# Layer 1's attention with scores turned round: keys on the partitions, exponentials in place, no transposes of probabilities

## The chip, the cores and the metric

The kernel runs on one core of a Trainium2 chip. The metric is the device time of one execution in microseconds (us), the median of several runs. A core has five engines, each of which works through its own instructions in order and waits for the others by semaphores: PE (matrix products, whose weight loads the profile lists apart as PEld), DVE (vector work), ACT (functions such as the exponential), POOL (a second vector engine) and SP (issues most DMA transfers here). Products land in PSUM, eight banks of 512 float32 columns on 128 partitions; everything else lies in SBUF.

## What is computed

Two layers over 1024 latent tokens (a grid of 16 x 64) and 256 context tokens, 1024 features wide, in float32. Layer 0 mixes by a gated MLP and a neighbourhood attention, layer 1 by a grouped-query attention, and each layer ends in a gated MLP with a short convolution. The change lies in layer 1's attention alone:

```python
def gqa_attend(q, k, v):
    bn, lq, hq, dh = q.shape
    hkv = k.shape[2]
    qg = q.reshape(bn, lq, hkv, hq // hkv, dh)
    s = jnp.einsum('bqhgd,bkhd->bhgqk', qg, k).astype(jnp.float32) * (dh ** -0.5)
    p = jax.nn.softmax(s, axis=-1).astype(v.dtype)
    return jnp.einsum('bhgqk,bkhd->bqhgd', p, v).reshape(bn, lq, hq * dh)
```

There are 16 query heads, 4 key/value heads and 64 features a head. The queries are the 1024 latent tokens, the keys the 1024 latent and the 256 context tokens, 1280 in all. Queries and keys have been normalised and rotated before.

## The kernel before

**Operands.** `odd_in` projects the tokens and writes queries, keys and values to DRAM. A query or key is kept as a sum of two numbers of the shorter type that PE takes at its fast rate (`F32R`), hi and lo. `qP` holds, for each head, the 64 hi features on partitions 0 to 63 and the 64 lo features on partitions 64 to 127. `kP` holds a first set in which both halves of the partitions are the key's hi part (`k1`), and a second in which both are its lo part (`k2`). So the product of q with `k1` plus the product of q with `k2` is the whole product of sums. `load_keys` brings `k1`, `k2` and the values `Vs` of one key/value head to SBUF: two heads near the end of `odd_in`, two at the beginning of the attention. `load_q` brings four query heads for 256 tokens.

**Tiles.** `odd_attn` goes through 128 tiles. A tile is one head and 128 queries, with the queries on the partitions: four stretches `p` of 256 queries, 16 heads in each, two tiles `q` for each head. Step n of the loop writes, in this order and with the matrix, vector and scalar engines bound to it (`in_order`):

- `scores` of tile n: for 512, 512 and 256 keys one product with `k1` and one with `k2` (line 1605); a copy of each piece to SBUF on DVE that also yields its maximum (line 1607); then the maximum of the three (line 1611), one exponential over all 1280 columns on ACT that also yields their sum (line 1612), and on POOL the reciprocal of that sum as a power (line 1613) and a diagonal matrix of the reciprocals (line 1619).
- `turns` of tile n - 3: ten transposes of 128 x 128 on PE (line 1634) and three copies out of PSUM, two on ACT and one on DVE (line 1636), which set the keys on the partitions.
- a quarter of the `values` of an earlier pair of heads: products of the turned probabilities with `Vs` (line 1651), in plain float32, which the trace lists as two records a product. Before the last quarter, `sums` multiplies a matrix of ones with the diagonals (line 1663), which sets each query's reciprocal on the 64 partitions of its head, and after it DVE multiplies the values by them (line 1654) and SP stores the result to `yT1`.

PSUM is split into four banks for scores, three for transposes and sums, and one for values.

**Beside it.** `down_sums` (called `ts`) prepares sums of layer 1's last weights: 11 times it loads two pieces into one tile, subtracts four times on POOL (line 611) and stores the tile. A step of it is taken at every second tile; the tile has one buffer. Near the end, at tile 118 and the seven after it, `out_load` brings the finished half of `yT1` back and splits it on POOL (lines 407 and 408) for the output projection that follows (lines 317 to 319).

Of the kernel before, what the change touches and what calls it, by code (L numbers as in the profile page):

```python
# [9 lines left out]
F32 = mybir.dt.float32  # L10
# [7 lines left out]
P = 128  # L18
# [37 lines left out]
class Net:  # L56
# [1515 lines left out]
    def load_keys(self, pool, kv):  # L1572
        res = []
        for tag, off in (("k1", 0), ("k2", 4)):
            x = self.t(pool, [P, S], f"{tag}_{kv}", 1, F32R)
            self.nc.sync.dma_start(x.bitcast(F32), self.kP[:, off + kv])
            res.append(x)
        x = self.t(pool, [P, NT, 64], f"Vs_{kv}", 1)
        self.nc.sync.dma_start(x, self.vP[:, kv])
        self.KV[kv] = (*res, x)  # L1580
# [6 lines left out]

    def odd_attn(self, es):
        nc, tc = self.nc, self.tc
        with tc.tile_pool(name="ga", reuse_waits="tile", bufs=2) as gp, self.banks(turn=4, one=3, out=1):  # L1590

            def scores(tl):

                pt = tl["pt"] = self.t(gp, [P, S], "pt", 6)
                mm = self.t(self.sp, [P, 3], "mm", 6)
                ng = self.t(self.sp, [P, 1], "ng", 6)
                sm = self.t(self.sp, [P, 1], "sm1", 6)
                ri = self.t(self.sp, [P, 1], "ri", 6)
                kv, q = tl["kv"], tl["q"]
                qs = tl["Q"][:, tl["h"] % 4, q * P:(q + 1) * P]  # L1600

                def keys(i, ps, c0, w):
                    ps = ps[:, :w]
                    for ki, kk in enumerate(self.KV[kv][:2]):
                        nc.tensor.matmul(ps, qs, kk[:, c0:c0 + w], start=(ki == 0), stop=(ki == 1))  # L1605

                    nc.vector.tensor_scalar(pt[:, c0:c0 + w], ps, 1.0, NEG, op0=ALU.mult, op1=ALU.max, accum_out=mm[:, i:i + 1])  # L1607

                def last():
                    keys(2, self.t(self.bt, [P, 512], "b1"), T, C)  # L1610
                    nc.vector.tensor_reduce(ng, mm, axis=AX.X, op=ALU.max, negate=True)  # L1611
                    nc.scalar.activation(pt, pt, AF.Exp, bias=ng, accum_out=sm)  # L1612
                    nc.gpsimd.tensor_tensor(ri, sm, self.mone, op=ALU.pow)  # L1613

                    x = tl["h"] % 2
                    if x == 0 and q == 0:
                        self.dg = self.t(gp, [P, 2, 256], "dg", 4)
                    tl["dg"] = self.dg
                    nc.gpsimd.tensor_scalar(self.dg[:, x, q * P:(q + 1) * P], self.ident, ri, None, op0=ALU.mult)

                return [lambda i=i: keys(i, self.t(self.bt, [P, 512], "b1"), 512 * i, 512) for i in range(2)] + [last]

            def turns(tl):

                x, q, pt = tl["h"] % 2, tl["q"], tl["pt"]
                if x == 0 and q == 0:
                    self.pT = self.t(gp, [P, 2, NT, 256], "pT", 2)
                pT = tl["pT"] = self.pT

                def batch(b0):  # L1630
                    m = min(4, NT - b0)
                    tb = self.bank()
                    for i in range(m):
                        nc.tensor.transpose(tb[:, i * P:(i + 1) * P], pt[:, (b0 + i) * P:(b0 + i + 1) * P], self.ident)  # L1634
                    e = nc.vector.tensor_copy if b0 == 4 else nc.scalar.copy
                    e(pT[:, x, b0:b0 + m, q * P:(q + 1) * P], tb[:, :m * P].rearrange("p (a b) -> p a b", a=m))  # L1636

                return [lambda b0=b0: batch(b0) for b0 in (0, 4, 8)]

            def values(tl):  # L1640

                p, h, kv, pT = tl["p"], tl["h"], tl["kv"], tl["pT"]
                box = {}

                def part(i0, i1):
                    if i0 == 0:
                        box["po"] = self.t(self.by, [P, 512], "by")
                    po = box["po"][:, :256]
                    for i in range(i0, i1):
                        for x in range(2):  # L1650
                            nc.tensor.matmul(po[x * 64:x * 64 + 64], self.KV[kv][2][:, i, :], pT[:, x, i, :], start=(i == 0), stop=(i == NT - 1))  # L1651
                    if i1 == NT:
                        ya = self.t(gp, [P, 256], "ya", 4)
                        nc.vector.tensor_tensor(ya, po, box["rb"], op=ALU.mult)
                        nc.sync.dma_start(self.yT1[h // 2][:, p * 256:(p + 1) * 256], ya)

                def sums():

                    tb = self.bank()[:, :256]
                    for q in range(2):  # L1660
                        for x in range(2):
                            c = slice(q * P, (q + 1) * P)
                            nc.tensor.matmul(tb[x * 64:x * 64 + 64, c], self.ones, tl["dg"][:, x, c], start=True, stop=True)
                    box["rb"] = self.t(gp, [P, 256], "rb", 2)
                    nc.scalar.copy(box["rb"], tb)

                cuts = (0, 3, 5, 8, NT)
                return [(sums if b == NT else None, lambda a=a, b=b: part(a, b)) for a, b in zip(cuts, cuts[1:])]

            tiles = [dict(p=p, h=h, kv=h // 4, q=q, j=p * 16 + h) for p in range(4) for h in range(16) for q in range(2)]  # L1670
            pend, n0, Qn = [], None, self.Q
# [3 lines left out]
            for n in range(len(tiles) + 5):  # L1675
                sc, tu = [], []
                if n < len(tiles):
                    tl = tiles[n]
                    if n % 8 == 0:
                        Q = Qn  # L1680
                    if n % 8 == 3 and n + 5 < len(tiles):
                        nx = tiles[n + 5]
                        Qn = self.load_q(gp, nx["p"], nx["h"])
                    if n % 2:
                        self.steps(ts, 1)
                    if n in (1, 6):
                        self.load_keys(gp, 2 + n // 6)
                    if tl["p"] == 3 and tl["h"] == 11 and tl["q"] == 0:

                        self.es_g.close()  # L1690
                        xp = es.enter_context(tc.tile_pool(name="xq", reuse_waits="tile", bufs=1, side="right"))
                        xm = self.xm_tiles(xp)
                        n0 = n
                    if n0 is not None and n - n0 < 8:
                        self.out_load(xm, n - n0, self.yT1, 0, HF, self.t(gp, [P, 512], "raw", 1), "pp")
                    tl["Q"] = Q
                    sc = scores(tl)
# [119 lines left out]
```

## Time and profile before

| | us |
|---|---|
| three runs | 3074.65, 3075.59, 3079.21 |
| median | 3075.59 |
| the profiled execution | 3070.96 |
| its span, first to last instruction | 3069.2 |
| layer 1's attention, first score product to last value product | 1769.9 to 2279 |

A profile shows one execution. A row of a group names the line, the engine, the operation, what is written from what, the shape, the number of instructions, their busy time in us and the mean of one in ns; behind the bar at the right stands how long the engine had been idle before them, and what ended it. A row of the timeline begins with the start and the length in us; rows of the same kind that follow each other are merged, and "x8" gives their number. A row of windows gives the length of the stretch, then the busy time and number of instructions for PE, PEld, DVE, ACT and POOL, PE's granted clock as a share of the full one, the share of DMA time, and GB/s. PE's listed lengths include the way through the array, so that neighbours overlap; the distance of two starts tells what a product costs in a row.

### The profile page before, as it was taken

The numbers are of one execution on the slowest core, as the hardware profiler recorded it, in microseconds if no ns is written. First come the engines' busy times: TensorE is split into PE (matmuls) and PEld (weight loads), VectorE is DVE, ScalarE is ACT, GpSimd is POOL, SyncE is SP. The second block draws the span as 40 slices with busy tenths as digits, with TensorE's granted clock in tenths as the row PEclk, the third lists the DMA queues.
The fourth block names the chain that finished last, engine by engine and source line by source line (L and its number), as shares of the span: only waits on it lengthen the run. The fifth ranks groups of instructions, "written<-read, shape, count | busy, mean of one in ns | idle before, by whom it ended". The sixth has DMA issues, their size and how long they took to land. (4 is left out here: it accounts for less than half of the span.)

```text
span 3069.2 us, 45832 instructions
## 1 busy us (share of the span) xinstructions
PE 2926.8 (95%) x16819; PEld 2354.1 (77%) x16819; DVE 2127.8 (69%) x3397; ACT 1406.5 (46%) x2407; POOL 1439.8 (47%) x1532
## 2 busy tenths in 40 slices
PE   7999988998999999999989999999999899999997
PEld 6768956676888888878779977777777678888785
DVE  4441245468766666798997776666656988788998
ACT  4211156374433333344466566666636344444443
POOL 3541046446333333266665766433344744442767
PEclk9999999999999999999999999999999899999998
DMA  9685453363323322553154554200033122224542
GB/s 347 220 285 178 126 178 96 125 220 113 107 95 115 122 90 106 190 170 129 54 196 121 171 213 172 76 31 23 28 122 138 55 89 83 83 82 158 189 145 82
DMA packets 221120, 408.56 MB, mean 133 GB/s; under 512 B 27216, under 2 KB 119376, under 8 KB 212960
## 3 DMA queue, kind: packets, MB, share of 16 engines
q1 hardware_dynamic: 198192, 390.10, 37.1%
q10 hardware_dynamic: 22704, 15.55, 1.7%
q8 instruction: 132, 2.16, 0.3%
q14 instruction: 92, 0.75, 0.1%
HBM read 300.65 MB, written 104.92 MB: 132 GB/s over the span
## 5 line engine op out<-in xcount | busy, mean ns | idle before, releaser
L1607 DVE TENSOR_SCALAR_CACHE_REDUCE pt<-b 128x512 f32<-128x512 f32 (+1 forms) x384 | 229.7, 599 | 136.3 <-PE b L1605 134.9
L459 POOL TENSOR_TENSOR sw<-wraw,wraw 128x512 f32<-128x512 f32 x44 | 60.1, 1366 | 469.0 <-DVE wlo L122 469.0
L122 DVE TENSOR_TENSOR wlo<-wraw,whi 128x1024 fp32r<-128x1024 f32 (+1 forms) x160 | 213.4, 1338 | 84.7 <-ACT whi L116 83.9
L116 ACT CAST whi<-sw 128x1024 fp32r<-128x1024 f32 x88 | 92.2, 1048 | 338.1 <-PE by L497 241.3
L1605 PE MATMUL b<-k,Q 128*128 128x512 f32 (+1 forms) x768 | 244.8, 403 | 0.8 <-DVE pt L1607 0.8
L116 ACT CAST whi<-wraw 128x1024 fp32r<-128x1024 f32 (+1 forms) x160 | 157.3, 988 | 188.9 <-PE b L308 107.1
L1612 ACT ACTIVATE pt<-pt,ng 128x1280 f32<-128x1280 f32 x128 | 174.8, 1365 | 109.8 <-DVE ng L1611 107.6
L498 PE MATMUL by<-xb,wlo 128*128 128x512 f32 x528 | 209.9, 398 | 6.6 <-DVE wlo L122 6.6
L496 PE MATMUL by<-xb,whi 128*128 128x512 f32 x528 | 212.1, 402 | 3.3 <-DVE z L475 1.8
L475 DVE TENSOR_TENSOR z<-by,z 128x512 f32<-128x512 f32 x176 | 120.8, 687 | 133.9 <-POOL z L475 84.0
L497 PE MATMUL by<-xb,whi 128*128 128x512 f32 x528 | 210.3, 398 | 2.5 <-DVE xb L122 2.5
L122 DVE TENSOR_TENSOR xb<-xb,xb 128x512 fp32r<-128x512 f32 (+2 forms) x184 | 167.6, 927 | 23.4 <-ACT xb L116 20.6
L1634 PEld LDWEIGHTS b<-ident,pt 128*128 128x128 f32 x1280 | 154.7, 140 | 36.4 <-DVE pT L1636 1.4
L1634 PE MATMUL b<-ident,pt 128*128 128x128 f32 x1280 | 181.2, 272 | 0.5 <-ACT pT L1636 0.4
L116 ACT CAST xb<-xb 128x512 fp32r<-128x512 f32 (+2 forms) x184 | 103.2, 567 | 168.4 <-PE by L870 61.6
L122 DVE TENSOR_TENSOR wlo<-sw,whi 128x1024 fp32r<-128x1024 f32 x88 | 128.0, 1455 | 65.6 <-ACT whi L116 64.8
L611 POOL TENSOR_TENSOR ts<-ts 128x512 f32<-128x512 f32 x88 | 116.8, 1337 | 110.5 <-DMA ts<-in_w_down_dram 95.7
L1651 PE MATMUL by<-pT,Vs 128*64 128x256 f32 x1280 | 165.9, 389 | 0.0
L1613 POOL TENSOR_TENSOR ri<-sm,mone 128x1 f32<-128x1 f32 x128 | 72.6, 568 | 181.9 <-ACT pt L1612 134.6
L732 POOL TENSOR_TENSOR y<-y,wraw 128x512 f32<-128x512 f32 x72 | 115.1, 1620 | 85.4 <-DVE wraw L732 54.1
L1636 ACT COPY pT<-b 128x512 f32<-128x512 f32 (+1 forms) x256 | 120.7, 474 | 65.6 <-PE b L1634 64.0
L496 PE MATMUL by<-xm,whi 128*128 128x512 f32 x352 | 142.6, 405 | 6.8 <-ACT z L525 3.2
(302 smaller groups left out, 9146.7 us busy)
## 6 DMA issues: line engine op xcount, KB each, us to landing
wraw<-in_w_up_t_dram SPq DMA_DIRECT2D x89, 512.0 KB
awr<-in_w_ada_dram SPq DMA_DIRECT2D x44, 1024.0 KB
ts<-in_w_down_dram SPq DMA_DIRECT2D x44, 512.0 KB
tD<-ts SPq DMA_DIRECT2D x22, 1024.0 KB
xm<-tD SPq DMA_DIRECT2D x88, 256.0 KB
hid<-o SPq DMA_DIRECT2D x43, 512.0 KB
xm<-in_w_down_dram SPq DMA_DIRECT2D x66, 256.0 KB
xb<-hid SPq DMA_DIRECT2D x66, 256.0 KB
```

What stands on the lines that cost most here:

```text
L116: nc.scalar.copy(hi, src)
L122: nc.vector.tensor_tensor(lo, src, hi.bitcast(F32), op=ALU.subtract)
L475: add = lambda o, x, y, e=V: e.tensor_tensor(o, x, y, op=ALU.add)
L496: nc.tensor.matmul(o, W[0][:, k, :], hi[k], start=(k == 0), stop=False)
L497: nc.tensor.matmul(o, W[0][:, k, :], lo[k], start=False, stop=False)
L498: nc.tensor.matmul(o, W[1][:, k, :], hi[k], start=False, stop=(k == 3))
L1605: nc.tensor.matmul(ps, qs, kk[:, c0:c0 + w], start=(ki == 0), stop=(ki == 1))
L1607: nc.vector.tensor_scalar(pt[:, c0:c0 + w], ps, 1.0, NEG, op0=ALU.mult, op1=ALU.max, accum_out=mm[:, i:i + 1])
L1612: nc.scalar.activation(pt, pt, AF.Exp, bias=ng, accum_out=sm)
L1634: nc.tensor.transpose(tb[:, i * P:(i + 1) * P], pt[:, (b0 + i) * P:(b0 + i + 1) * P], self.ident)
L1636: e(pT[:, x, b0:b0 + m, q * P:(q + 1) * P], tb[:, :m * P].rearrange("p (a b) -> p a b", a=m))
L1651: nc.tensor.matmul(po[x * 64:x * 64 + 64], self.KV[kv][2][:, i, :], pT[:, x, i, :], start=(i == 0), stop=(i == NT - 1))
```

## The change

The unit of work becomes a block of four query heads (one key/value head `g`) and 128 queries: 32 blocks instead of 128 tiles. The score products are turned round: a chunk of 128 keys is the fixed operand, the four heads' queries (4 x 128 columns) stream through, and the result has the keys on the partitions, as the value products want it.

A maximum over the keys can no longer be taken from such a product. So `maxima` computes, for each head, the product of q with `k1` only, queries on the partitions, into three PSUM banks, and one reduction on DVE over 1280 columns gives the negated maximum. `rounded` copies the four to the shorter type on ACT; `shift` turns and spreads them over the partitions by four products with an identity, and ACT copies the upper half into `q2`, a second query operand whose lower half is q's hi part, loaded by a DMA of its own. `k2` now has its lo part on partitions 0 to 63, a row of ones on partition 64 and zeros below (two memsets on POOL). So the second score product adds lo times hi and takes off the maximum; lo times lo is left out. The exponential reads PSUM, has no bias and gives no sum.

The sum over the keys is formed from the ten chunks of exponentials: POOL adds chunks 0 to 4 (`first`, four additions), DVE adds 5 and 6 to 7 and 8 (`second`), then folds that, adds chunk 9 and POOL's part (`third`); two products with ones (`sums`) spread it over the 64 partitions of each head. DVE takes the reciprocal and multiplies (`result`). The transposes, their copies, the diagonals and POOL's powers are gone. PSUM is split into one buffer of three banks for the maxima, three banks for scores and shifts, two for values and sums.

Within a step the parts are written for four blocks: the block itself (`b`), the next two (`b1`, `b2`) and the one before (`last`). `ts` takes two steps a block; the load back for the output projection goes to blocks 29 to 31.

```diff
     def load_keys(self, pool, kv):
-        for tag, off in (("k1", 0), ("k2", 4)):
-            x = self.t(pool, [P, S], f"{tag}_{kv}", 1, F32R)
-            self.nc.sync.dma_start(x.bitcast(F32), self.kP[:, off + kv])
+        hi, lo = (self.t(pool, [P, S], f"{tag}_{kv}", 1, F32R) for tag in ("k1", "k2"))
+        self.nc.sync.dma_start(hi.bitcast(F32), self.kP[:, kv])
+        self.nc.sync.dma_start(lo[0:64].bitcast(F32), self.kP[0:64, 4 + kv])
+        self.nc.gpsimd.memset(lo[64:P].bitcast(F32), 0.0)
+        self.nc.gpsimd.memset(lo[64:65].bitcast(F32), 1.0)
...
+            def maxima(b, h):
+                ps = self.t(self.b2, [P, 1536], "b2")
+                for c, w in ((0, 512), (512, 512), (T, C)):
+                    nc.tensor.matmul(ps[:, c:c + w], b["q1"][:, h], self.KV[b["g"]][0][:, c:c + w], start=True, stop=True)
+                nc.vector.tensor_reduce(b["ng"][:, h:h + 1], ps[:, :S], axis=AX.X, op=ALU.max, negate=True)
...
+            def shift(b):
+                ps = self.t(self.bt, [P, 512], "b1")
+                for h in range(4):
+                    nc.tensor.matmul(ps[:, h * P:(h + 1) * P], b["mr"][:, h:h + 1].to_broadcast([P, P]), self.identr, start=True, stop=True)
+                nc.scalar.copy(b["q2"][64:P], ps[64:P].rearrange("p (h q) -> p h q", h=4))
+
+            def scores(b, k):
...
+                for i in range(2):
+                    nc.tensor.matmul(ps.rearrange("p (h q) -> p h q", h=4), self.KV[b["g"]][i][:, c], b[f"q{i + 1}"], start=(i == 0), stop=(i == 1))
+                nc.scalar.activation(b["pT"][:, k], ps, AF.Exp)
...
+            def sums(b):
+                for i in range(2):
+                    nc.tensor.matmul(out(b["po"][:, 256:], i), self.ones, two(b["acc"][:, 0], i), start=True, stop=True)
+
+            def first(b):
+                pT = b["pT"]
+                x = b["part"] = self.t(gp, [P, 512], "part", 2)
+                nc.gpsimd.tensor_tensor(x, pT[:, 0], pT[:, 1], op=ALU.add)
+                for k in (2, 3, 4):
+                    nc.gpsimd.tensor_tensor(x, x, pT[:, k], op=ALU.add)
+
+            def second(b):
+                b["acc"] = self.t(gp, [P, 2, 512], "acc", 2)
+                nc.vector.tensor_tensor(b["acc"], b["pT"][:, 5:7], b["pT"][:, 7:9], op=ALU.add)
+
+            def third(b):
+                x = b["acc"]
+                for y in (x[:, 1], b["pT"][:, 9], b["part"]):
+                    nc.vector.tensor_tensor(x[:, 0], x[:, 0], y, op=ALU.add)
+
+            def result(b):
+                rb = self.t(gp, [P, 256], "rb", 2)
+                nc.vector.reciprocal(rb, b["po"][:, 256:])
+                ya = self.t(gp, [P, 256], "ya", 4)
+                nc.vector.tensor_tensor(ya, b["po"][:, :256], rb, op=ALU.mult)
...
+            for h in range(4):
+                maxima(blocks[0], h)
+            rounded(blocks[0])
+            for h in range(2):
+                maxima(blocks[1], h)
+            shift(blocks[0])
+            for n in range(len(blocks) + 1):
...
+                if b2:
+                    begin(b2)
+                self.steps(ts, 2)
...
+                if b:
+                    scores(b, 0)
+                if last:
+                    second(last)
+                    values(last, 5, NT)
+                if b1:
+                    maxima(b1, 2)
+                if last:
+                    third(last)
+                if b:
+                    for k in (1, 2, 3, 4):
+                        scores(b, k)
+                    first(b)
+                if b1:
+                    maxima(b1, 3)
+                    rounded(b1)
+                if b:
+                    scores(b, 5)
+                if last:
+                    sums(last)
+                if b:
+                    values(b, 0, 5)
+                if b1:
+                    shift(b1)
+                if b2:
+                    maxima(b2, 0)
+                if last:
+                    result(last)
+                if b:
+                    for k in (6, 7, 8, 9):
+                        scores(b, k)
+                if b2:
+                    maxima(b2, 1)
```

More of the change, by code (lines that the diff above doesn't have):

```diff
@@ L1572, in load_keys @@
     def load_keys(self, pool, kv):
-        res = []
-        for tag, off in (("k1", 0), ("k2", 4)):
-            x = self.t(pool, [P, S], f"{tag}_{kv}", 1, F32R)
-            self.nc.sync.dma_start(x.bitcast(F32), self.kP[:, off + kv])
-            res.append(x)
+        hi, lo = (self.t(pool, [P, S], f"{tag}_{kv}", 1, F32R) for tag in ("k1", "k2"))
[3 more added lines that the diff above has]
+        self.nc.gpsimd.memset(lo[64:65].bitcast(F32), 1.0)
         x = self.t(pool, [P, NT, 64], f"Vs_{kv}", 1)
         self.nc.sync.dma_start(x, self.vP[:, kv])
-        self.KV[kv] = (*res, x)
+        self.KV[kv] = (hi, lo, x)
     def load_q(self, pool, p, h, bufs=2):
@@ L1589, in odd_attn @@
         nc, tc = self.nc, self.tc
[L1590 to L1671, printed above, removed]
@@ L1674, in odd_attn @@
             pinned.enter_context(self.in_order(nc.tensor, nc.vector, nc.scalar))
[L1675 to L1697, printed above, removed]
-                if 0 <= n - 3 < len(tiles):
-                    tu = turns(tiles[n - 3])
-                before, after = pend.pop(0) if pend else (None, None)
-                if before:
-                    before()
-                for f in [x for y in zip(sc[:2], tu[:2]) for x in y] + tu[2:] + sc[2:] if sc and tu else sc + tu:
-                    f()
-                if after:
-                    after()
-                if 0 <= n - 3 < len(tiles) and tiles[n - 3]["h"] % 2 and tiles[n - 3]["q"] == 1:
-                    pend += values(tiles[n - 3])
@@ L1709, in odd_attn @@
-            for before, after in pend:
-                if before:
-                    before()
-                after()
+            xp = None
+            begin(blocks[0])
+            begin(blocks[1])
+            self.load_keys(gp, 2)
+            for h in range(4):
[5 more added lines that the diff above has]
+            for n in range(len(blocks) + 1):
+                b, b1, b2, last = was(n), was(n + 1), was(n + 2), was(n - 1)
+                if n == 0:
+                    self.load_keys(gp, 3)
+                if b2:
+                    begin(b2)
+                self.steps(ts, 2)
+                if n == 29:
+                    self.es_g.close()
+                    xp = es.enter_context(tc.tile_pool(name="xq", reuse_waits="tile", bufs=1, side="right"))
+                    xm = self.xm_tiles(xp)
+                if n >= 29:
+                    for k in range(3 * (n - 29), min(KD, 3 * (n - 28))):
+                        self.out_load(xm, k, self.yT1, 0, HF, self.t(gp, [P, 512], "raw", 2), "pp")
+                if b:
[31 more added lines that the diff above has]
+                    maxima(b2, 1)
```

31 lines of the change are left out of this document (added).

## The prediction

> **What bounds the kernel now.** I read the busy times on the page first, then the engine windows over layer 1's attention (1770 to 2280 us), then PE's timeline inside it.
>
> ```profile
> PE 2926.8 (95%) x16819; PEld 2354.1 (77%) x16819; DVE 2127.8 (69%) x3397; ACT 1406.5 (46%) x2407; POOL 1439.8 (47%) x1532
> 1769.80:2280.00 510.20, 504.66 (x3661) 373.43 (x3660) 338.14 (x1066) 315.43 (x555) 222.84 (x321) 0.99 0.24 85
> 1950.00:2050.00 100.00, 100.00 (x744) 73.91 (x742) 68.58 (x218) 63.48 (x112) 31.03 (x53) 1.00 0.08 25
> ```
>
> The reader is to see that PE (first figure behind the length) is idle for 5.5 us of this stage and not at all in its middle, with DVE and ACT near two thirds and DMA at 0.08. So PE's own work is the bound, and every microsecond taken from PE counts until another engine makes PE wait. PE's timeline:
>
> ```profile
> 2000.65 0.61 PE L1663 MATMUL b<-dg,ones 128*64 128x128 f32 x8
> 2001.18 0.73 PE L1605 MATMUL b<-k,Q 128*128 128x512 f32 x2
> 2001.75 0.60 PE L1634 MATMUL b<-ident,pt 128*128 128x128 f32 x4
> 2002.11 0.71 PE L1605 MATMUL b<-k,Q 128*128 128x512 f32 x2
> 2002.65 0.82 PE L1634 MATMUL b<-ident,pt 128*128 128x128 f32 x6
> 2003.23 0.48 PE L1605 MATMUL b<-k,Q 128*128 128x256 f32 x2
> 2003.63 1.08 PE L1651 MATMUL by<-pT,Vs 128*64 128x256 f32 x8
> 2004.65 0.74 PE L1605 MATMUL b<-k,Q 128*128 128x512 f32 x2
> ...
> 2007.11 1.52 PE L1651 MATMUL by<-pT,Vs 128*64 128x256 f32 x12
> 2008.55 0.73 PE L1605 MATMUL b<-k,Q 128*128 128x512 f32 x2
> ```
>
> Starts count here, since listed lengths overlap. A tile (one head, 128 queries) takes 3.47 us with 8 value records and 3.90 with 12; with one group of sums (0.53) four tiles take about 15.2, and 32 such blocks 486 us. The transposes are 0.36 + 0.58 = 0.94 of each tile. Value records: 1.02 for 8, 1.44 for 12, so 0.107 each and 0.17 for a group.
>
> **The change, part by part.** PE first. The price of a long run of the score kind of product (512 and 256 columns) stands in other stages:
>
> ```profile
> 2254.54 0.39 PE L317 MATMUL by<-whi,xm 128*128 128x512 f32 x1
> ...
> 2257.34 0.39 PE L317 MATMUL by<-whi,xm 128*128 128x512 f32 x1
> ...
> 1768.73 0.28 PE L319 MATMUL by<-whi,xb 128*128 128x256 f32 x1
> ...
> 1769.44 0.28 PE L319 MATMUL by<-whi,xb 128*128 128x256 f32 x1
> 1769.56 0.46 PE L1513 MATMUL b<-identr,xb 128*128 128x128 f32 x4
> ```
>
> Twelve products lie between the first two (0.234 each), six between the others (0.118). A new block (four heads, 128 queries) has 20 score products, 4.68; maxima 8 x 0.234 + 4 x 0.118 = 2.34; 40 value records in two groups, 4.62; sums, 4 records, 0.43; shift about 0.4; two switches back, 0.2. Together 12.7 against 15.2: the transposes' 3.76 go, the maxima's 2.34 come, and longer runs save the rest. The shift's four products are bounded by four transposes of that width (0.46, the last row) and eight sums records (0.53), and below by 0.2; 0.4 is near both. Scores read q with a stride; their pairs now take up to 0.57, so 0.234 to 0.285 a product, and I take the long run. The high end adds some 0.5 a block to the path below.
>
> The other engines:
>
> ```profile
> L1636 DVE COPY pT<-b 128x512 f32<-128x512 f32 x128 | 87.8, 686 | 12.0 <-PE b L1634 12.0
> L1636 ACT COPY pT<-b 128x512 f32<-128x512 f32 x128 | 73.7, 575 | 13.5 <-PE b L1634 12.0
> L1654 DVE TENSOR_TENSOR ya<-by,rb 128x256 f32<-128x256 f32 x32 | 13.6, 425 | 18.2 <-PE by L1651 14.5
> L1312 DVE TENSOR_REDUCE ng<-b 128x1 f32<-128x256 f32 x16 | 6.0, 420 | 2.0 <-PE b L1302 2.0
> L1323 ACT ACTIVATE pt<-sc,ng 128x640 f32<-128x640 f32 x64 | 52.5, 824 | 7.6 <-DVE ng L1309 7.6
> L1279 POOL MEMSET bias<- 128x256 f32 x12 | 3.2, 310 | 114.4 <-DMA qD<-t 102.2 <-DMA VD<-h 6.6 <-issue 5.6
> 2002.85 0.69 DVE L1607 TENSOR_SCALAR_CACHE_REDUCE pt<-b 128x512 f32<-128x512 f32 x1 [0.20 <-PE b L1605]
> 2503.39 1.22 DVE L575 TENSOR_TENSOR o<-o,o 128x1024 f32<-128x1024 f32 x1
> 2833.14 0.69 DVE L122 TENSOR_TENSOR wlo<-xm,wlo 128x512 fp32r<-128x512 f32 x1
> 2833.74 0.69 DVE L122 TENSOR_TENSOR whi<-xm,whi 128x512 fp32r<-128x512 f32 x1
> ```
>
> ACT: ten exponentials of 512 at 0.58 (the copy; at most 0.82, the 640 row), the shift's copy and a tiny one: 6.6 to 9 us a block, hidden under PE's 12.7. `rounded` waits for the fourth maximum, and exponentials 5 to 9 queue behind it; the values before the shift cover that. DVE: a maximum over 1280 columns is 420 + 4 x 266 = 1.48 (266 is 686 less 420); 1.73 by the 0.69-us row's 1.35 ns an element. `second` is 1.22, `third` three adds of 0.68 that follow from each other, 2.1. An add that waits for nothing starts 0.08 before the last one's end (0.60 apart, 0.69 long). [...] DVE sums to 10.1, under PE. POOL loses its power and diagonal work and gains four adds a block. Its eight memsets are 1.55 each by the 256-wide row; `k2` is needed only after the lead-in, which hides the first two pairs; uncovered, 3 to 6 us once. SP issues 32 small q2 loads and twice the stores, and a block's loads stand behind the stores of the block before, which wait for `result`; DMA at 0.08 hides them, since q is wanted some 10 us after issue. If it were late, the third and fourth maxima of a block would wait for it.
>
> **The path within a block.** PE runs in a written order, so the added wait of `sums` for `third` holds back all behind it: five value chunks, the shift, two maxima, scores 6 to 9. Round the loop: sums 0.6 with the group, values 2.14, shift 0.5, maximum 0.59, scores 1.87, maximum 0.59, score 0.47, values 2.41, maximum 0.59, hand-over 0.20 (the row above), reduction 1.40, `third` 2.10, hand-over 0.1: **13.55 us**. PE idles 0.85 of it in front of `sums`.
>
> Then what POOL does meanwhile. POOL's four adds (`first`) read chunks 0 to 4 as ACT makes them. Let t be the end of the third maximum's products on PE. Score 1 is streamed at t + 0.47, its exponential done at t + 1.25, POOL starts at t + 1.35; `third` is ready at t + 0.20 + 1.40 = t + 1.6. Both read two operands each. How such adds share the time shows late in the kernel:
>
> ```profile
> 2904.69 1.74 POOL L681 TENSOR_TENSOR xb<-xb,a 128x512 f32<-128x512 f32 x1
> 2905.20 1.78 DVE L122 TENSOR_TENSOR wlo<-xm,wlo 128x512 fp32r<-128x512 f32 x1
> 2906.38 1.74 POOL L681 TENSOR_TENSOR xb<-a,a 128x512 f32<-128x512 f32 x1
> 2906.90 1.77 DVE L122 TENSOR_TENSOR xb<-a,xb 128x512 fp32r<-128x512 f32 x1
> 2908.08 1.74 POOL L681 TENSOR_TENSOR a<-a,xb 128x512 f32<-128x512 f32 x1
> ```
>
> The same DVE add takes 1.78 here and 0.69 above: one add of POOL and one of DVE go by turns, 1.70 a pair. [...] By whole lengths a pair would be 1.29 + 0.60 = 1.89, and the total some 8 us more than by the row.
>
> So `third` waits until POOL's first add is through (1.29 long in the next fence, t + 2.6), and two more pairs follow: its last add starts at t + 6.0 and ends at t + 6.7 instead of t + 3.7. That is 3.0 us, PE's stall grows to about 3.9, and the block takes **16.55**. Whether POOL waits for its chunk alone or for all chunks written ahead of it is read from the weight sums, whose two subtractions read two halves of one tile:
>
> ```profile
> 1829.75 1.29 POOL L611 TENSOR_TENSOR ts<-ts 128x512 f32<-128x512 f32 x1 [4.20 <-DMA ts<-in_w_down_dram]
> 1831.82 1.28 POOL L611 TENSOR_TENSOR ts<-ts 128x512 f32<-128x512 f32 x1 [0.79 <-DMA ts<-in_w_down_dram]
> ```
>
> The second waits again, for its own half: a reader waits for its piece. In every other one of the first 22 blocks these subtractions stand ahead of `first` and wait for a load issued in that block (4.20 above), so `first` comes after `third`; there I take half of one encounter, 14.1.
>
> **Lead-in.** Six maxima share one PSUM buffer: 0.59 + 0.20 + 1.48 + 0.1 = 2.37 each. PE is nearly idle then, and this is its clock (last figure but two of a window) in such a gap:
>
> ```profile
> 1773.72 0.51 PE L1513 MATMUL b<-identr,xb 128*128 128x128 f32 x4 [2.01 <-DVE xb L122]
> 1776.43 0.72 PE L1513 MATMUL b<-identr,xb 128*128 128x128 f32 x4 [2.20 <-DVE xb L122]
> ...
> 1774.00:1776.00 2.00, 0.23 (x3) 0.09 (x2) 1.34 (x4) 0.99 (x2) 0.85 (x1) 0.81 0.99 257
> 1776.00:1778.00 2.00, 0.78 (x5) 0.62 (x5) 1.10 (x4) 0.59 (x1) 0.00 (x0) 0.50 0.80 271
> ```
>
> With some products at half clock I take 16 us up to the first score (14 to 18).
>
> **Sum.** After: 16, then 10.5 for the first block (nothing to finish), 10 x 14.1, 21 x 16.55, and -3 for maxima that the last blocks lack, net of the last block's finish, which the output projection covers as it does now: 512. Before: 486 + 5.5 idle = 491.5. The difference is **+20.5 us**. The profiled execution took 3070.96 us for a span of 3069.2, so it becomes 3091.5; it lies 4.6 under the median of the three runs, 3075.59, on which I put the forecast: **3096**. Its own range is 3082 (shift and lead-in at their low ends, no encounter in the ten blocks) to 3121 (score pairs, reductions and lead-in at their high ends).
>
> **Rivals.**
> 1. *No turns, so faster.* If POOL's first add starts only past t + 3.0, when `third` has issued its last add, nothing collides: every block takes 13.55, the stage 16 + 10.5 + 31 x 13.55 - 3 = 443.5, so 48 less: 3028. [...] For it: ACT's exponentials could be slower than the copy, or POOL could wait for chunk 4 (t + 3.1). Against: the half-tile rows. It decides where the mean block passes (491.5 - 16 - 10.5 + 3) / 31 = 15.1.
> [...]
> 3. *The stall lowers the clock.* A stall of 3.9 is as long as the gap before 0.50 in the rows above (two waits with four products between). If sums and values then ran at half clock, 2.7 us come on top in 21 blocks: 3153.
> 4. *About even*: one collision instead of three, near 15.1 a block.
>
> That the transposes stay is no case; the diff leaves no call of them.
>
> **Chances.** Forecast 0.30, dear reciprocal 0.20, clock 0.04: slower 0.54. No turns 0.36: faster. Even 0.10. About 0.2% (6 us) is what a measurement can tell from no change. The range 3030 to 3130 reaches into both sides and leaves out the cheap end of rival 1 and rival 3.
>
> **What would show it.** PE: blocks of 12.7 us of work, a stall of 3 to 4 in front of the sums released by DVE's last add in late blocks (right), or under 1 (rival 1). DVE: adds of `third` at 1.7 while POOL's run, or 0.68. [...] PEclk under 1.0 in mid-stage means rival 3. I am wrong from the ground up if products of the new shapes are not 0.234, or if the stage downstream moves.

## The result and the profile after

| | us, median of the runs | range |
|---|---|---|
| before | 3075.17 | 3074.65 to 3079.21 |
| after | 3177.12 | 3174.36 to 3179.81 |

The ratio is 1.0329, with an interval from 1.0311 to 1.0346: the change is slower, as forecast, but by 102 us, not by 20, and 47 us outside the range. The profiled execution of after took 3177.34 us for a span of 3175.6. The stages before the attention and after it keep their lengths; the difference lies between 1767 and 2372 us.

The busy row of the page of after, and further down its row of the granted clock (40 slices of 79.4 us, in tenths; the attention is slices 23 to 30):

```profile
PE 2923.6 (92%) x15795; PEld 2300.6 (72%) x15795; DVE 2220.0 (70%) x2661; ACT 1289.5 (41%) x2247; POOL 1491.7 (47%) x1412
...
PEclk9999999999999999999999888888899899999999
```

PE has a thousand instructions fewer than before and is busy as long, and in seven of the attention's eight slices its clock reads 8. The windows of after say it more closely:

```profile
2050.00:2150.00 100.00, 82.56 (x430) 52.77 (x431) 68.97 (x52) 30.99 (x63) 31.50 (x21) 0.85 0.08 24
2150.00:2250.00 100.00, 82.66 (x444) 53.35 (x443) 74.58 (x56) 33.67 (x68) 30.35 (x21) 0.88 0.11 32
```

Where PE was busy for 100 us of 100 before, at 1.00, it is busy for 82.6, at 0.85 to 0.88 (last figure but two). One block on PE's timeline of after, from the third maximum's products to the shift:

```profile
2098.54 0.85 PE L1612 MATMUL b<-k,Q 128*128 128x512 f32 x3
2099.23 0.40 PE L1632 MATMUL b<-Q,k 128*128 128x512 f32 x1
...
2101.94 0.40 PE L1632 MATMUL b<-q,k 128*128 128x512 f32 x1
2105.81 1.12 PE L1648 MATMUL by<-acc,ones 128*64 128x256 f32 x4 [3.47 <-DVE acc L1665]
2106.71 4.48 PE L1644 MATMUL by<-pT,Vs 128*64 128x256 f32 x20
2111.12 1.00 PE L1623 MATMUL b<-identr,mr 128*128 128x128 f32 x4
```

Two things are to be seen: PE stands 3.47 us in front of the sums, and what follows is slow. The sums and the five value chunks fill 2105.81 to 2111.12, 5.3 us, while in the same block the other five chunks were listed at 2.38. DVE and POOL beside it, in after:

```profile
2099.47 1.48 DVE L1613 TENSOR_REDUCE ng<-b 128x1 f32<-128x1280 f32 x1
2100.87 1.55 DVE L1665 TENSOR_TENSOR acc<-acc 128x512 f32<-128x512 f32 x1
2102.52 1.57 DVE L1665 TENSOR_TENSOR acc<-acc,pT 128x512 f32<-128x512 f32 x1
2104.19 1.56 DVE L1665 TENSOR_TENSOR acc<-acc,part 128x512 f32<-128x512 f32 x1
```

```profile
2100.58 1.29 POOL L1654 TENSOR_TENSOR part<-pT 128x512 f32<-128x512 f32 x1 [11.87 <-ACT pT L1633]
2101.95 4.93 POOL L1656 TENSOR_TENSOR part<-part,pT 128x512 f32<-128x512 f32 x3
```

These are the forecast's turns: DVE's three adds take 1.55 to 1.57 beside POOL's and start some 1.65 apart, near the 1.70 of the forecast's row and under the 1.89 of whole lengths. With t = 2099.23, the end of the third maximum's products, POOL begins at t + 1.35 and the third sum ends at t + 6.5 (forecast t + 1.35 and t + 6.7). The waits of PE in after, over the attention (line waited at, releaser, sum in us, times, longest):

```profile
PE by L1648 <- DVE acc L1665: 102.0, 30, 3.5
```

So the stall comes in 30 of 32 blocks (not in the last two), not in 21. The first group of sums starts at 1807.7 and the last of 32 at 2372.0: 18.2 us a block. Groups of after, over the attention:

```profile
L1669 DVE RECIPROCAL rb<-by 128x256 f32<-128x256 f32 x29 | 50.7, 1748 | 0.0
L1613 DVE TENSOR_REDUCE ng<-b 128x1 f32<-128x1280 f32 x128 | 190.0, 1484 | 153.5 <-PE b L1612 153.5
L1633 ACT ACTIVATE pT<-b 128x512 f32<-128x512 f32 x320 | 170.4, 601 | 121.9 <-PE b L1632 121.8
```

The reduction is the 1.48 us of the forecast and the exponential lies between its bounds. The reciprocal is 1.75 us, four times the 0.425 of the multiply of its shape. Whether that matters, and what the clock costs, no single trace settles.

### The profile page after: what moved, and what is told of

Its sections match the earlier page's. It is cut to its first block, busy times and chain, and to the rows that moved or that the text cites. A ratio compares the mean times of both kernels' runs of the same rounds, so it can differ in the third digit from the quotient of the medians.

```text
span 3175.6 us, 42948 instructions
## 1 busy us (share of the span) xinstructions
PE 2923.6 (92%) x15795; PEld 2300.6 (72%) x15795; DVE 2220.0 (70%) x2661; ACT 1289.5 (41%) x2247; POOL 1491.7 (47%) x1412
## 4 chain that ended last, share of the span: by engine, by line
PE 63%; DVE 19%; POOL 5%; DMA 5%; issue 5%; ACT 3%; ACTq 1%; SPq 0%; DVEq 0%; POOLq 0%
PE by L496 8%; PE by L497 8%; PE by L498 8%; DVE acc L1665 4%; PE by L1644 4%; DVE ng L1613 3%; PE by L871 2%; PE by L869 2%; PE by L870 2%; PE by L319 2%; PE by L318 2%; PE by L317 2%; DVE rb L1669 2%; PE b L306 2%; PE b L310 2%
## 5 line engine op out<-in xcount | busy, mean ns | idle before, releaser
L1613 DVE TENSOR_REDUCE ng<-b 128x1 f32<-128x1280 f32 x128 | 190.0, 1484 | 153.5 <-PE b L1612 153.5
L1633 ACT ACTIVATE pT<-b 128x512 f32<-128x512 f32 x320 | 170.4, 601 | 121.9 <-PE b L1632 121.8
L1644 PE MATMUL by<-pT,Vs 128*64 128x256 f32 x1280 | 201.8, 476 | 0.0
L1654 POOL TENSOR_TENSOR part<-pT 128x512 f32<-128x512 f32 x32 | 42.7, 1335 | 292.3 <-ACT pT L1633 292.3
L1644 PEld LDWEIGHTS by<-pT,Vs 128*64 128x64 f32 x1280 | 113.3, 174 | 83.5 <-issue 60.7
L1656 POOL TENSOR_TENSOR part<-part,pT 128x512 f32<-128x512 f32 x96 | 146.6, 1527 | 6.1
L496 PE MATMUL by<-xm,whi 128*128 128x512 f32 x352 | 142.5, 405 | 7.3 <-ACT z L525 3.2
L497 PE MATMUL by<-xm,whi 128*128 128x512 f32 x352 | 141.5, 402 | 0.0
L498 PE MATMUL by<-xm,wlo 128*128 128x512 f32 x352 | 141.4, 403 | 0.1
```

The source lines that it names most:

```text
L496: nc.tensor.matmul(o, W[0][:, k, :], hi[k], start=(k == 0), stop=False)
L497: nc.tensor.matmul(o, W[0][:, k, :], lo[k], start=False, stop=False)
L498: nc.tensor.matmul(o, W[1][:, k, :], hi[k], start=False, stop=(k == 3))
L1613: nc.vector.tensor_reduce(b["ng"][:, h:h + 1], ps[:, :S], axis=AX.X, op=ALU.max, negate=True)
L1633: nc.scalar.activation(b["pT"][:, k], ps, AF.Exp)
L1644: nc.tensor.matmul(out(b["po"][:, :256], i), self.KV[b["g"]][2][:, k], two(b["pT"][:, k], i), start=(k == 0), stop=(k == NT - 1))
```

## The experiments

The theory after the result: POOL's adds delay the third sum in every block, the stall of 3.5 us that this makes in front of the sums lowers PE's clock, and the two together are the loss. Rivals: the reciprocal; a clock that falls because of what PE computes, not because it waits; a loss that is not the turns'. Each block length below is the distance from the first group of sums to the last, divided by 31.

### What the reciprocal costs

```diff
-                nc.vector.reciprocal(rb, b["po"][:, 256:])
+                nc.vector.tensor_copy(rb, b["po"][:, 256:])
```

> A copy stands in for the reciprocal, so the values are multiplied by the sums instead of divided by them. Theory that the reciprocal (1.75 us) stands on the path: 1.3 us less a block, 30 x 1.3 = 39 us, about 3138. Theory that PE's values between the last two maxima hide it: within 5 us of 3177.

Measured: 3177.70 us (1.0333, 1.0315 to 1.0350), the time of after. The copy takes 0.41 us on DVE; the 1.34 us saved are won nowhere, since DVE then waits for PE before two of its four reductions (0.18 and 0.92 us in mid-stage). The reciprocal is out.

### Taking the turns away

First by order alone: POOL begins with the chunk that is ready last.

```diff
-                nc.gpsimd.tensor_tensor(x, pT[:, 0], pT[:, 1], op=ALU.add)
-                for k in (2, 3, 4):
+                nc.gpsimd.tensor_tensor(x, pT[:, 4], pT[:, 3], op=ALU.add)
+                for k in (2, 1, 0):
```

> POOL's four additions in reverse order of chunks (4 and 3 first, then 2, 1, 0), so that the first of them waits for chunk 4. Theory of the turns: POOL now starts about 1.8 us later, when third has issued its last addition; third's additions fall from 1.56 to 0.69 us, PE's wait in front of the sums from 3.5 to about 0.9 us, the clock in mid-stage comes back to 1.0, a block takes 13.6 us instead of 18.5, and the time is 3177 - 30 x 4.9 = about 3030 us. Theory of the dear reciprocal: the loop goes round DVE whatever POOL does, and the time stays within 10 us of 3177. If only the turns went and the low clock had another cause: a block of 15.6, about 3090 us.

Measured: 3076.73 us, 1.0004 of before (0.9994 to 1.0013): 100 us gone, and 47 us short of what was expected. DVE's timeline and POOL's in this kernel show why:

```profile
1973.31 0.68 DVE L1665 TENSOR_TENSOR acc<-acc 128x512 f32<-128x512 f32 x1
1974.09 0.69 DVE L1665 TENSOR_TENSOR acc<-acc,pT 128x512 f32<-128x512 f32 x1
1974.89 1.56 DVE L1665 TENSOR_TENSOR acc<-acc,part 128x512 f32<-128x512 f32 x1
```

```profile
1974.46 1.45 POOL L1654 TENSOR_TENSOR part<-pT 128x512 f32<-128x512 f32 x1 [8.90 <-ACT pT L1633]
```

Two adds are short; POOL's first add still meets the last one. PE's stall falls to 1.76, and the clock is 1.00 from 1950 to 2150 us: a shorter stall no longer lowers it. The block is 14.9.

Then by leaving POOL's adds out, with everything else in its place, except that a copy stands for the reciprocal again:

```diff
-                x = b["part"] = self.t(gp, [P, 512], "part", 2)
-                nc.gpsimd.tensor_tensor(x, pT[:, 0], pT[:, 1], op=ALU.add)
-                for k in (2, 3, 4):
-                    nc.gpsimd.tensor_tensor(x, x, pT[:, k], op=ALU.add)
...
-                for y in (x[:, 1], b["pT"][:, 9], b["part"]):
+                for y in (x[:, 1], b["pT"][:, 9], b["pT"][:, 9]):
...
-                nc.vector.reciprocal(rb, b["po"][:, 256:])
+                nc.vector.tensor_copy(rb, b["po"][:, 256:])
```

> Leaves out the weight sum of chunks 0 to 4 and the division: POOL adds nothing in the loop but its subtractions of weight sums, DVE's third sum has three adds as before and at the same place, and a copy stands for the reciprocal (which by itself changed nothing). Nothing of the order of PE changes. If the turns alone start it all, the adds take about 0.7 us, the third sum ends 2.6 us earlier or more, the stall before the sums is 0.9 us or less, the clock stays at 1.00, and the block is 13.5 us: 3177 - 29 x 5.0 = about 3032 us. If the clock falls for another reason than the stall (what PE computes, the products over 64 rows of ones), only the 3.0 us of turns go: 3177 - 29 x 3.0 = about 3090. If turns were not the cause of the long adds: 3177.

Measured: 3050.96 us (0.9915, 0.9892 to 0.9939). PE's timeline of this kernel in mid-stage:

```profile
1972.78 0.65 PE L1648 MATMUL by<-acc,ones 128*64 128x256 f32 x4 [0.77 <-DVE acc L1661]
...
1986.54 0.65 PE L1648 MATMUL by<-acc,ones 128*64 128x256 f32 x4 [0.76 <-DVE acc L1661]
```

The distance of the two is 13.76, against the forecast's path of 13.55, with a stall of 0.77 against 0.85. So without turns the loop is what the forecast drew, and the 126 us under after come from POOL's four adds, turns and low clock together (the copy alone won nothing above). Most of the 19 us above the expected time lies in the eleven blocks up to 1973 us, where POOL's weight sums still meet the second and the third sum (stalls up to 2.65, blocks of 15 us); the mean block is 14.2.

### Is it the wait that lowers the clock?

The stall was filled with products whose result is overwritten; nothing else moves. With 24 of them:

```diff
                 if last:
+                    for _ in range(24):
+                        hi = self.KV[last["g"]][0]
+                        nc.tensor.matmul(last["po"][:, 256:], hi[:, :P], hi[:, :256], start=True, stop=True)
                     sums(last)
```

> 24 useless products of 256 columns (2.8 us) on PE in front of the sums, into the place that the sums overwrite; the wait for third is left. Theory that the wait lowers the clock: sums and five value chunks go back from 4.7 to 2.7 us, a block from 18.5 to about 16.6, and the time falls by 30 x 2 = 60 us to about 3117, though PE does more. Theory that the clock is low for another reason (or that the slow values have nothing to do with it): no gain, 3177 us or more.

Measured: 3122.64 us (1.0153, 1.0138 to 1.0169). 768 products more, and 54.5 us less. PE's timeline of this kernel, then one of its windows:

```profile
1976.74 3.03 PE L1725 MATMUL by<-k 128*128 128x256 f32 x24
1980.53 0.65 PE L1648 MATMUL by<-acc,ones 128*64 128x256 f32 x4 [0.76 <-DVE acc L1665]
1981.01 2.33 PE L1644 MATMUL by<-pT,Vs 128*64 128x256 f32 x20
```

```profile
2050.00:2150.00 100.00, 95.96 (x630) 71.12 (x629) 81.50 (x61) 36.62 (x73) 36.84 (x24) 1.00 0.11 33
```

The value chunks are back at 2.33 and the clock at 1.00. The turns are all there, and the mean block is 16.55 us (16.5 in mid-stage), the forecast's figure for a block with turns at full clock. So the clock follows the wait, and it costs 18.2 - 16.55 = 1.65 us a block.

How long must the wait be? The same with 12 products and with 6 (`range(12)`, `range(6)`):

> 12 useless products of 256 columns (about 1.5 us, half of the filler before) ahead of the sums, and nothing else changed: about 2.0 us of the 3.5 us stall is left, and all of the filler lies in it. If the clock needs a stall of more than about 2 us to fall, it stays at 1.00 as with 24 products and the time is the same, about 3120 us. If shorter waits lower it too, the sums and the five value chunks stay at some 4 us instead of 2.7 in most blocks: 3150 or more. If only the work done between matters, in proportion to it: about half way, 3148.

> 6 useless products of 256 columns (about 0.75 us) ahead of the sums: about 2.75 us of the stall is left (3.47 without filler, about 2.0 with 12, 0.76 with 24). With 12 the clock mostly held and the time was 3133, with none it fell in every block, 3177. If a wait of 2.75 us lowers it as one of 3.47 does: about 3177 less what of the 54 us the shorter slow stretch gives, 3165 or more. If the limit lies between 2.75 and 3.47: about 3133.

| filler products | wait left, us | clock, 2050 to 2150 us | block, us | time, us (ratio to before) |
|---|---|---|---|---|
| 0 | 3.47 | 0.85 | 18.2 | 3177.1 (1.0329, 1.0311 to 1.0346) |
| 6 | 2.8 | 0.86 | 17.9 | 3179.0 (1.0326, 1.0297 to 1.0355) |
| 12 | 2.07 | 0.98 | 16.7 | 3132.9 (1.0194, 1.0177 to 1.0211) |
| 24 | 0.7 | 1.00 | 16.55 | 3122.6 (1.0153, 1.0138 to 1.0169) |

PE's timeline with 12 products, two blocks in a row:

```profile
2046.81 0.89 PE L1648 MATMUL by<-acc,ones 128*64 128x256 f32 x4 [2.08 <-DVE acc L1665]
2047.47 3.83 PE L1644 MATMUL by<-pT,Vs 128*64 128x256 f32 x20
...
2064.99 0.65 PE L1648 MATMUL by<-acc,ones 128*64 128x256 f32 x4 [2.07 <-DVE acc L1665]
2065.48 2.33 PE L1644 MATMUL by<-pT,Vs 128*64 128x256 f32 x20
...
2098.00 0.89 PE L1648 MATMUL by<-acc,ones 128*64 128x256 f32 x4 [2.06 <-DVE acc L1665]
```

With the same wait the clock falls in one block and holds in the next: the value chunks are slow in 9 of the 30 blocks, often every third. With 2.8 they are slow in all blocks from 1915 to 2300 us, as with 3.47. In this loop the limit is near 2 us and not a length alone: from 1944 to 2200 us the slow blocks come every 51.2 us (2046.81 and 2098.00 above).

The granted clock itself shows where that distance comes from. In before and after all its changes, 33 and 95, lie within 12 ns of one grid of 3413 ns (in after one low stretch goes from 2087.96 to 2091.37). The 51.2 us are 15.0 such windows, and two blocks of after, from 2050.09 to 2087.64, are 11.0 of them. Stretches of this grid with 12 products, two beside the wait at 2046.81 and two beside the wait at 2064.99:

```profile
2043.67:2047.09 3.42, 1.34 (x13) 1.06 (x14) 3.32 (x3) 0.00 (x0) 3.26 (x3) 1.00 0.00 0
2047.09:2050.50 3.41, 3.41 (x20) 1.95 (x18) 1.06 (x1) 0.69 (x2) 0.78 (x1) 0.50 0.00 0
...
2060.74:2064.15 3.41, 2.19 (x16) 1.87 (x14) 3.20 (x3) 0.39 (x1) 3.25 (x3) 1.00 0.00 0
2064.15:2067.57 3.42, 2.58 (x24) 1.63 (x24) 2.19 (x2) 0.69 (x2) 1.84 (x2) 1.00 0.00 0
```

The first wait lies within one window, which leaves PE busy for 1.34 us of it, and the next window runs at 0.50. The second is cut by a window's edge (2.19 and 2.58 us busy), and the clock holds. From 1767 to 2375 us of the four runs of the table the clock fell behind each of the 67 windows at full clock in which PE was idle for 1.91 us or more, and behind none of the 531 with 1.88 us or less. So whether a wait of 2.1 us counts depends on how much of it lies in one window, and one of 1.76 never counted here. Idle time is not the whole rule: in the versions below that move the sums, the clock also fell behind windows with 1.46 us idle and held behind others with up to 1.77; why is left open. The loss is not a proportion: 12 of 24 products bring back 44 of the 54 us.

### The ten blocks that were to be free

The forecast held that in ten blocks weight-sum subtractions stand ahead of POOL's adds and put them off. POOL is not bound to the written order, and the planner set it otherwise. POOL's timeline of after, in an early block:

```profile
1969.84 1.30 POOL L1654 TENSOR_TENSOR part<-pT 128x512 f32<-128x512 f32 x1 [7.98 <-ACT pT L1633]
1971.22 3.25 POOL L1656 TENSOR_TENSOR part<-part,pT 128x512 f32<-128x512 f32 x2
...
1975.49 1.27 POOL L611 TENSOR_TENSOR ts<-ts 128x512 f32<-128x512 f32 x1 [1.01 <-DMA ts<-in_w_down_dram]
```

The subtraction stands behind three of the four adds, and it is there that it waits for its load. Here POOL is bound to the written order:

```diff
-            pinned.enter_context(self.in_order(nc.tensor, nc.vector, nc.scalar))
+            pinned.enter_context(self.in_order(nc.tensor, nc.vector, nc.scalar, nc.gpsimd))
```

> The changed kernel with POOL's instructions held in the order in which the loop writes them, so that in the first 22 blocks the two subtractions of weight sums stand ahead of the partial sum, as the forecast took it. Nothing else differs. If the forecast was right about such blocks (every other one waits for its load, POOL's partial sum comes after DVE's third sum, half an encounter), ten blocks fall from 18.2 to about 14.1 us: 3177 - 10 x 4.1 = 3136. If the subtractions take turns with the third sum just as the partial sum does, or delay the partial sum until the sums wait for it, nothing is won: 3170 or more.

Measured: 3184.09 us (1.0353, 1.0338 to 1.0369), block 18.3. POOL's timeline of this kernel:

```profile
1827.13 2.49 POOL L611 TENSOR_TENSOR ts<-ts 128x512 f32<-128x512 f32 x2
1838.99 1.30 POOL L1654 TENSOR_TENSOR part<-pT 128x512 f32<-128x512 f32 x1 [9.38 <-ACT pT L1633]
1840.37 4.93 POOL L1656 TENSOR_TENSOR part<-part,pT 128x512 f32<-128x512 f32 x3
1845.26 2.61 POOL L611 TENSOR_TENSOR ts<-ts 128x512 f32<-128x512 f32 x2
```

In the written order the subtractions wait for a load in the first and the third block alone (the stall of the third is 2.64). From the fourth on their load is there when POOL gets to them, they run at once behind the block before, and 9.4 us later the partial sum starts where it always does. So no block was ever free.

### A version without the stall

The sums may stand behind the five value chunks, which need nothing from the third sum.

```diff
-                if last:
-                    sums(last)
                 if b:
                     values(b, 0, 5)
+                if last:
+                    sums(last)
```

> The five value chunks of the block are put in front of the sums of the block before; POOL and DVE are left as they are, so the additions still go by turns. Theory: the values (2.3 us) cover two thirds of the wait, about 1.3 us of it stays, the clock holds, and the values leave the loop from the sums to the next third: 16.55 - 2.1 = about 14.4 us a block, 3177 - 30 x 4.1 = about 3054 us. Theory of the dear reciprocal: the loop round DVE also loses the values, but keeps 1.3 us for the reciprocal; about 15.5 us a block, 3087 us. If PE's wait is not what counts: 3177.

Measured: 3111.61 us (1.0120, 1.0093 to 1.0147), 58 us over the expectation. PE's timeline of this kernel:

```profile
1972.05 2.38 PE L1644 MATMUL by<-pT,Vs 128*64 128x256 f32 x20
1975.62 0.65 PE L1648 MATMUL by<-acc,ones 128*64 128x256 f32 x4 [1.19 <-DVE acc L1665]
1977.25 0.66 PE L1623 MATMUL b<-identr,mr 128*128 128x128 f32 x4 [0.97 <-ACT mr L1617]
1977.75 1.25 PE L1612 MATMUL b<-k,Q 128*128 128x512 f32 x3
1978.80 0.63 PE L1632 MATMUL b<-Q,k 128*128 128x512 f32 x1
1979.22 0.63 PE L1632 MATMUL b<-q,k 128*128 128x512 f32 x1
```

The one wait has become two, since the fourth maximum's reduction stands behind the third sum on DVE, and the shift waits for it through `rounded`. The score products after them start 0.42 apart, not 0.234: 1.19 and 0.97 us with 0.65 of work between lowered the clock as one longer wait did, in 19 of the 30 blocks. Where the clock holds, a block takes 15.4 us, still 1.0 over the 14.4 expected, which is the second wait. Both edits together:

> Both edits of the two runs before together: POOL's adds begin with the chunk that comes last, and the five value chunks stand ahead of the sums. If the turns and the wait for the third sum are all that is left above PE's 12.7 us a block, the 2.33 us of value products now cover the 1.76 us stall, the reduction behind the third sum is about 1.8 us earlier than with the sums alone later, and the block falls from 14.7 to about 12.9 us: 3076 - 29 x 1.8 = about 3024 us. If the one turn of POOL's first add with the last add of the third sum still matters through the reduction behind it, a wait of some 0.5 us is left: about 3038. If DVE's own order is the bound (reductions 5.9, reciprocal 1.75, multiply 0.42, sums 1.2 and 3.0: 12.3 us of 12.9) waits appear before the first maxima of the next block and the time is 3050 or more.

Measured: 3046.04 us (0.9911, 0.9896 to 0.9926), 8 us above the second of the three cases. The sums wait for nothing in mid-stage; a wait of 0.6 to 1.0 us in front of the shift is left in 30 blocks, 21.9 us in all, and a block takes 13.6 us in mid-stage. For the last turn, POOL's part became chunks 5 to 1 (DVE takes 6 to 9, then 0), behind chunk 5; the cut shows the edit against after, and the sums stay behind the value chunks:

```diff
-                nc.gpsimd.tensor_tensor(x, pT[:, 0], pT[:, 1], op=ALU.add)
-                for k in (2, 3, 4):
+                nc.gpsimd.tensor_tensor(x, pT[:, 5], pT[:, 4], op=ALU.add)
+                for k in (3, 2, 1):
...
-                    first(b)
...
                     scores(b, 5)
+                    first(b)
```

> POOL's partial sum is of chunks 5, 4, 3, 2, 1 in that order and is placed behind chunk 5's product; DVE's second sum takes chunks 6 to 9 and its third sum chunk 0; the sums stand behind the five value chunks. No add of POOL can begin before DVE's third sum is done, so no turn is left (three adds of about 0.7 us). If the last turn cost something in the run with both edits, this is 0.9 us a block under it, at PE's 12.7 us: about 3015 us. If PE's work already covered it: the same as that run within 5 us.

Measured: 3042.73 us (0.9897, 0.9882 to 0.9912), the same as the run before within its bound. In mid-stage there is no turn left and PE is busy for 100.00 of 100 us, blocks 12.9 apart, so the last turn had cost 0.7 us a block there; most of what is missing from 3015 lies in the first eleven blocks, where four subtractions a block meet the second and third sums (15.4 us each from 1887 to 1964). So the weight sums were spread over 22 blocks, two subtractions in each:

```diff
-                self.steps(ts, 2)
+                self.steps(ts, 1)
```

(with `down_sums` giving way for layer 1 only between the two pairs of subtractions and after the store), once with POOL free and once bound as above.

> The fastest version so far (partial sum of chunks 5 to 1 behind chunk 5, sums behind the five value chunks) with half as many steps of the weight sums in a block: two subtractions in each of 22 blocks in place of four in each of eleven, POOL's order left to the scheduler. In that version the eleven blocks take some 15.4 us because subtractions take turns with DVE's second and third sum, the others 12.9. If two fit behind the partial sum, ahead of DVE's third: 3043 - 11 x 2.4 = about 3017. If each block now meets one pair of turns: 22 blocks lose about 1 us, 3038 to 3043.

> The same with POOL held in the written order, the two subtractions ahead of the partial sum of the next block, so behind that of the block before (5.3 us from the end of chunk 5; 2.6 us more end about when DVE's third sum begins). If the order is what matters: 3043 - 11 x 2.4 = about 3017. If the weights' loads come late, the subtractions move into the third sum and delay the partial sum: 3043 or more.

Measured: 3043.35 us free (0.9894, 0.9879 to 0.9909), so nothing won: the subtractions still stand four to a block of 15.4 us there, done by 1958 us. Bound: **3026.25 us** (0.9838, 0.9823 to 0.9852), below both kernels, 1.6% under before. One block on DVE in the bound version, then POOL's row of the subtractions before it, PE's row of the fourth maximum, and a window of this kernel in the early part:

```profile
1855.08 1.74 DVE L1662 TENSOR_TENSOR acc<-pT 128x1024 f32<-128x1024 f32 x1
1856.74 1.48 DVE L1615 TENSOR_REDUCE ng<-b 128x1 f32<-128x1280 f32 x1
1858.15 0.68 DVE L1667 TENSOR_TENSOR acc<-acc 128x512 f32<-128x512 f32 x1
1858.86 0.69 DVE L1667 TENSOR_TENSOR acc<-acc,pT 128x512 f32<-128x512 f32 x1
1859.65 0.69 DVE L1667 TENSOR_TENSOR acc<-acc,part 128x512 f32<-128x512 f32 x1
```

```profile
1854.46 3.52 POOL L611 TENSOR_TENSOR ts<-ts 128x512 f32<-128x512 f32 x2
```

```profile
1858.28 0.85 PE L1614 MATMUL b<-k,Q 128*128 128x512 f32 x3 [0.28 <-DVE ng L1615]
```

```profile
1850.00:1950.00 100.00, 98.27 (x598) 65.07 (x598) 85.67 (x75) 44.81 (x90) 65.81 (x48) 1.00 0.39 132
```

The subtractions end at 1857.98 and the third sum begins at 1858.15: they now meet only the second sum. PE is busy for 98 us of 100 at full clock. The second sum is not free: it takes 1.74 us instead of 1.22, the third maximum's reduction behind it ends later, and the fourth maximum's products wait for the buffer that this reduction frees. A block takes 13.43 us up to 2076 us, where the subtractions end, and 12.92 behind. Some 20 blocks of 0.5 us are 10 us, about what the run lies above the expected 3017.

## Why the prediction was wrong

**The direction and its mechanism were right.** POOL's `first` goes by turns with DVE's `third`, from t + 1.35, and the block with turns is 16.55 us at full clock: forecast, and measured with the stall filled (16.5 in mid-stage). Without POOL's adds the path is 13.76 (forecast 13.55), without any wait PE's block is 12.9 (12.7).

**The step that failed first: rival 3, "the stall lowers the clock", chance 0.04.** It was the case, and the sum of the forecast has no term for it. Its price was worked out as 2.7 us in 21 blocks, 57 us; filling the stall brings back 54.5, which is 1.8 us in each of 30 blocks. That the two totals agree is luck: the price of a block was too high and the number of blocks too low. The rows that it was read from, a clock of 0.50 behind two gaps of some 2 us with four products between, were the right ones, and no row of before spoke against them; the chance had nothing to stand on. The runs show in the place of that chance that one wait of 2.8 us in a block was enough, that one of about 2.1 was enough in 9 of 27 cases, and that the clock fell behind each window of 3413 ns in which PE was idle for 1.91 us or more.

**The second: the ten blocks at 14.1,** where "these subtractions stand ahead of `first` and wait for a load". In after they stand among POOL's adds or behind them, where they wait for a load seven times (3.2 us at most), and bound to that order they wait in two blocks alone. Ten blocks at 16.55 in place of 14.1 are 24.5 us.

Together, from the forecast: 3096 + 24.5 (ten blocks) + 54.5 (clock) + 1.5 (lead-in 17.5 us in place of 16) = 3176.5, against 3177.1. That it closes so well is partly luck: with the stall filled the first ten blocks take 17.3 us, the middle ones 16.5 and the last two 13.6 and 12.3, and only their mean is 16.55.

**Rival 2, a dear reciprocal.** It had a chance of 0.20. Its price of a reciprocal was the author's estimate, which no run shows, and so was the 0.425 us of a multiply that the forecast's 10.1 us of DVE count for it. In their place after shows 1.75 us, so that DVE's 10.1 become 11.4, still under PE's 12.7. A loop round DVE is then hand-over 0.2, three reductions of 1.40, reciprocal 1.75, multiply 0.35, `second` 1.14, `third` 2.10, hand-over 0.1 and PE's sums, values, shift and maximum 3.83: 13.7 us, a tie with the 13.55 of PE's path and not more. The trace of after fits that: from the reduction at 2112.79 to the end of the next third sum DVE waits for nothing. With a copy in its place DVE waits for PE instead, and nothing changes; whether a longer one would cost is not shown by any run.

**Rival 1** gave 3028, and the bound version, without turns and with the sums moved, takes 3026. That is luck: the rival reckoned 31 blocks of 13.55 with the sums in their old place. The run that stands for it, without POOL's adds, has 13.76 in mid-stage and took 3051, since the weight sums still lengthen the first eleven blocks. The point from which it decides, POOL's first add past t + 3.0, was also right: with the order reversed POOL starts at t + 2.8, too early for one of three adds, and one turn is left.

**Also right or harmless:** score products 0.234 apart, strided or not; the loads of q and the memsets, for neither of which PE waits in after.

## What to carry to other kernels

When a change puts a wait into the engine that is the bound, price the wait and also what that engine does after it: here the slow stretch behind a 3.5-us wait cost about half as much as the wait. Before adding work to POOL, look at what DVE does in the same microseconds (its adds of 512 columns went from 0.69 to 1.56 us here), and set the place of POOL's instructions by their data or by a bound order, since it decides what they meet and what waits for that. A wait can be tested cheaply by filling it with work that nobody needs: if the time falls, as by 54.5 us with 24 products here, the wait cost more than its length.

## What the runs showed of the hardware

- PE's clock changes between 1.00 and 0.50 on a grid of 3413 ns in before (33 changes) and after (95). With 0, 6, 12 and 24 filler products it fell behind every window with PE idle for 1.91 us or more (67) and behind none with 1.88 or less (531); with the sums moved the two overlap, from 1.46 to 1.77.
- So it fell behind nearly every single wait of 2.8 us or more in a block of 18 us, behind 9 of 27 waits of about 2.1, and not behind those of 1.76 between 1950 and 2150 us. Two waits of 1.19 and 0.97 with 0.65 us of products between them lowered it in 19 of 30 blocks.
- A two-operand add of DVE on 512 columns goes from 0.69 to 1.56 us beside POOL's, one of 1024 columns from 1.22 to 1.74. The reduction from PSUM stays at 1.48 us beside the same POOL adds.
- The reciprocal of 128 x 256 from PSUM takes 1.75 us, where a copy of that shape takes 0.41.
